# State space tables from low powers and multiples of 16, for four pairs at once, in place of a doubling per two pairs

## The chip, the cores and the metric

The kernel is one program on one core of one Trainium2 chip. The metric is the device time of one execution in microseconds. Three runs of the kernel before took 2755.88, 2739.55 and 2752.0 us; their median, 2752.0 us, is the time to compare with.

## What is computed

The input is a residual stream x of 1024 tokens by 2048 columns, in float32, and the reference passes it through two layers. Layer 0 has one input projection, eight gating heads, eight heads of stick-breaking attention and an output projection. Layer 1 is a diagonal complex state space (S5) with a gated linear unit. Each layer is modulated by a conditioning vector and normed before and after.

Only layer 1's state space matters for the change. It has 64 groups of 16 channels with 64 complex states each:

```
a   = exp(lam * dt)                                   # per group and state, complex
h_t = a * h_(t-1) + (coef * b) u_t                    # scan over the 1024 tokens
y_t = Re(c h_t) + d_skip * u_t
```

The kernel works in chunks of 8 tokens, 128 of them. From one chunk to the next a state is multiplied by a^8, which is a magnitude and a turn e8 = exp(i * angle). The scan over chunks runs on real numbers after the states have been turned back; so it needs, for every state, the table of turns e8^n for n = 0 to 127, as cosine and sine. This table, called `et`, is what the change computes in another way.

## The kernel before

**The whole.** A scheduler sets the order of every engine's instructions from the order in which they are written, their dependencies and priorities; each engine then works through its own list strictly in order. TensorE (PE) is busy nearly all the time. Each projection is a float32 product made of three matmuls: `load_w` splits a raw weight chunk into a high part, which ScalarE (ACT) copies (`whi`, L180), and a low part, which VectorE (DVE) subtracts (`wlo`, L181), and `mm3` multiplies them (L206 to L208).

**Layer 0** loops over eight heads h (L623). A head has a projection `v`, every second one a projection `bz`, then `qk`, the attention, and `uz`. Attention (L540) is a chain of short steps for each block of 128 queries: scores `z` on PE, three functions on ACT, add (L557), masks on GpSimd (POOL, L559 and L572), a scan (L563) and a subtraction (L569) on DVE, an exponential on ACT, transposes on PE, their copy `wT` on DVE (L578), and the product `oT` on PE (L580). The attention of a head runs beside the `v` projection of the next.

**The preparation of layer 1** is spread through layer 0. The generator `s5_prep` is started after the attention of head 3, and from then on a loop takes its steps, by `NPREP`: 3 in head 3, 4 each in heads 4 to 6, 1 in head 7. As the scheduler sets them, they run beside the projections of heads 4 to 7. A step makes the matrices of two pairs of groups, so that there are 16 steps. In each:

- POOL loads `br`, `bi` and, in every second step, `cl`; DVE makes `bbr`, `bbi` and the block matrix `bd`.
- POOL multiplies them by powers of a (`gm`, `ga`, L1143 and L1146): `Tr` and `Ti`, then `cAr` and `cAi`. DVE ends `cAi` (L1210).
- `write_wb` transposes `Tr` and `Ti` of one pair on PE (`wb_ps`, L1215); DVE (L1217) and ACT (L1218) copy them into `wb`, and SP stores that. It is called for the first pair early, and for the second after the table.
- PE multiplies `bd` with `cAr` and `cAi` (`k_ps`, L1228 and L1230); DVE writes it beside 128 zeros into `kst`, and SP stores both halves into `kk_d`.
- DVE makes the table `et` by doubling: from m entries the next m are those times e8^m (`em`), 6 instructions for each of 7 levels, and 5 more to square `em` for each of the first 6. SP stores it by four DMAs into `et_d`.

All tiles of the preparation have one buffer; so the next step's `et` waits until the four DMAs of the last have read it.

Of the kernel before, what the change touches and what calls it, by code (L numbers as in the profile page):

```python
# [13 lines left out]
ALU = mybir.AluOpType  # L14
PSUM = bass.MemoryType.PSUM
# [10 lines left out]
class TableOrder:  # L26
    """Keeps the ScalarE functions that need different tables in separate runs."""

# [35 lines left out]
def hybrid_trunk(ctx: ExitStack, tc: tile.TileContext, x, c, ln_pre_g, ln_post_g, w_mod, b_mod,  # L64
# [27 lines left out]

# [1 line left out]
    cat_d = dram.tile([16, 128, L], F32, name="cat_d")  # L94
# [9 lines left out]

# [1 line left out]
    ident = const.tile([128, 128], F32, name="ident")  # L106
# [33 lines left out]
    def rstd_from(ss, n, cnt, pool, name):  # L140
        """1/sqrt(ss/cnt + eps) of a [128, n] tile: exp(-log/2), then one Newton step."""
        r = pool.tile([128, n], F32, tag=name, name=name)
        v = pool.tile([128, n], F32, tag=name + "v", name=name + "v")
        t = pool.tile([128, n], F32, tag=name + "t", name=name + "t")
        V.tensor_scalar(out=v, in0=ss, scalar1=1.0 / cnt, scalar2=EPS, op0=ALU.mult, op1=ALU.add)
        tab.act(r, v, AF.Ln)
        tab.act(r, r, AF.Exp, scale=-0.5)
        V.tensor_tensor(out=t, in0=r, in1=r, op=ALU.mult)
        V.tensor_tensor(out=t, in0=t, in1=v, op=ALU.mult)
        V.tensor_scalar(out=t, in0=t, scalar1=-0.5, scalar2=1.5, op0=ALU.mult, op1=ALU.add)  # L150
        V.tensor_tensor(out=r, in0=r, in1=t, op=ALU.mult)
        return r

    def col_sums(ps, acc, n):
        """[128, n*128] partial sums -> [128, n] PSUM columns."""
        for i in range(n):
          with hi_prio():
            T.matmul(ps[:, i:i + 1], acc[:, i * 128:(i + 1) * 128], ones, start=True, stop=True)
# [16 lines left out]

# [1 line left out]
    RAW, SUB = 1024, 512  # L177
# [5 lines left out]
    def load_raw(parts, ncols, dma=dma):  # L183
        """parts: (k, first column, DRAM slice [128, k, n]) -> raw tile [128, RAW]."""
        raw = wp.tile([128, RAW], F32, tag="wraw", name="wraw")
        rv = raw.rearrange("p (k n) -> p k n", n=ncols)
        for k, c0, src in parts:
            dma(out=rv[:, k:k + src.shape[1], c0:c0 + src.shape[2]], in_=src)
        return raw
# [3 lines left out]
    def load_w(parts, ncols, eng=V, raw=None, dma_=dma):  # L193
        """Yields the weight chunk in parts of SUB elements, split."""
        if raw is None:
            with hi_prio():
                raw = load_raw(parts, ncols, dma_)
        for i in range(RAW // SUB):
            with hi_prio():
                h = wp.tile([128, SUB], F32R, tag="whi", name="whi")  # L200
                lo = wp.tile([128, SUB], F32R, tag="wlo", name="wlo")
                split(h, lo, raw[:, i * SUB:(i + 1) * SUB], eng)
            yield h.rearrange("p (k n) -> p k n", n=ncols), lo.rearrange("p (k n) -> p k n", n=ncols)
# [6 lines left out]
    def gemm(nk, ncols, src, banks, evac, name, pre=None, eng=V):  # L210
        """src(k0, k1): parts of the weight rows; banks: (width, f), f(k, w_hi, w_lo) -> operands.

        k outermost, so that every weight chunk is used once; in the last chunk bank by bank."""
        ps = [mm_tile(name) for _ in banks]
# [17 lines left out]

# [1 line left out]
    w7 = w_in_ab[0].rearrange("(k p) (s n) -> p k s n", p=128, s=7)  # L234
# [25 lines left out]

# [1 line left out]
    # h^T starts without the shift: its part of the first projections is a bias, and the shift is added to h^T later.  # L262
    first = ((6, None), (3, 4), (0, 2))
# [156 lines left out]

# [1 line left out]
    with pool("pa") as pa, pool("pu") as pu_, pool("pst") as pst, pool("pat", 2) as pat, ExitStack() as pm_stack:  # L422
# [15 lines left out]
        def bias_first():  # L438
            """The shift's part of the first projections."""
            for gi, (s0, s1) in enumerate(first):  # L440
# [25 lines left out]
        def mod_chunk(layer, n0):  # L466
            """512 columns of silu(c) @ w_mod, as partial sums over partitions."""
            acc = pm.tile([128, 512], F32, tag="macc", name="macc")
# [31 lines left out]
        def sgu_scale(h):  # L500
            """Per-token norm of gelu(v) over the head, in the exp/log run."""
            av = st["av"]
# [92 lines left out]
        def gate_a(h):  # L595
            """Gates of gating head h, with gelu of the next head's v."""
            tab.begin("silu")
# [66 lines left out]

# [1 line left out]
    h1h = [None, None]  # L666
# [3 lines left out]
    def pairs(ap, k0, cols):  # L670
        """Rows KORD[k0], KORD[k0 + 1] of ap [128, k, n], in one part if adjacent."""
        a, b = KORD[k0], KORD[k0 + 1]
        if b == a + 1:
            return [(0, 0, ap[:, a:a + 2, cols])]
        return [(i, 0, ap[:, k:k + 1, cols]) for i, k in enumerate((a, b))]
# [82 lines left out]

# [1 line left out]
    wi = w_in_ssm[0].rearrange("(k p) n -> p k n", p=128)  # L760
# [130 lines left out]

# [1 line left out]
    yTh = big_tile(1, [128, 8, L], F32R, "yTh")  # L893
# [34 lines left out]

# [1 line left out]
    with pool("pd") as pd:  # L930
# [55 lines left out]
def s5_prep(nc, tc, tab, const, pst, ps_t, ps_o, ident, dma, lam_re, lam_im, b_re, b_im, c_re, c_im,  # L986
            d_skip, log_dt, wb_d, wc_d, kk_d, et_d):
    """Matrices of the state space for chunks of 8 steps; a generator, two pairs of groups per step.

    Rows (g2 p): the 64 states of the two groups of a pair."""  # L990
    V, S, G, T = nc.vector, nc.scalar, nc.gpsimd, nc.tensor
# [4 lines left out]
    def small(shape, name):  # L996
        cnt[0] += 1
        return pools[0].tile(shape, F32, tag=f"s5{name}", name=f"s5{name}{cnt[0]}")
# [152 lines left out]
    s5b = ExitStack()  # L1151
    pools[0] = s5b.enter_context(tc.tile_pool(name="s5b", bufs=1, reuse_waits="tile"))
    for bq in range(32 // NP):
        p0 = bq * NP
        b, g0 = p0 // 4, (p0 % 4) * 2
        psl = slice(p0, p0 + NP)
        if p0 % 4 == 0:
            cl = small([128, 2, 64], "cl")
# [67 lines left out]
        for r in range(NP):  # L1226
# [4 lines left out]
                     start=False, stop=True)  # L1231
            kst = small([32, 256], "kst")
            V.memset(kst[:, 0:128], 0.0)
            V.tensor_copy(kst[:, 128:256], pk)
            V.scalar_tensor_tensor(out=kst[:, 128:144], in0=eye2, scalar=dcol[:, p0 + r:p0 + r + 1],
                                   in1=kst[:, 128:144], op0=ALU.mult, op1=ALU.add)
            dma(out=kk_d[2 * (p0 + r):2 * (p0 + r) + 2].rearrange("g c x -> (g c) x"), in_=kst)
        et = small([128, NP, 2, 128], "et")
        em = small([128, 2, NP, 1], "em")
        tc_ = small([128, NP, 64], "tc")  # L1240
        V.memset(et[:, :, 0, 0:1], 1.0)
        V.memset(et[:, :, 1, 0:1], 0.0)
        V.tensor_copy(em[:, 0, :, 0], e8[:, 0, psl])
        V.tensor_copy(em[:, 1, :, 0], e8[:, 1, psl])
        m = 1
        while m < 128:
            emr, emi = (em[:, i].to_broadcast([128, NP, m]) for i in range(2))
            o_r, o_i = et[:, :, 0, m:2 * m], et[:, :, 1, m:2 * m]
            s_r, s_i = et[:, :, 0, 0:m], et[:, :, 1, 0:m]
            tt = tc_[:, :, 0:m]  # L1250
            mul(o_r, s_r, emr)
            mul(tt, s_i, emi)
            add(o_r, o_r, tt, ALU.subtract)
            mul(o_i, s_r, emi)
            mul(tt, s_i, emr)
            add(o_i, o_i, tt)
            if 2 * m < 128:
                e_r, e_i = em[:, 0], em[:, 1]
                x_, y_, w_ = tc_[:, :, 0:1], tc_[:, :, 1:2], tc_[:, :, 2:3]
                mul(x_, e_r, e_r)  # L1260
                mul(y_, e_i, e_i)
                mul(w_, e_r, e_i)
                add(e_r, x_, y_, ALU.subtract)
                add(e_i, w_, w_)
            m *= 2
        write_wb(1)
        for top in range(2):
# [33 lines left out]
```

## Time and profile before

| | |
|---|---|
| median of the runs, and their bounds | 2752.0 us, 2739.55 to 2755.88 |
| span of the profiled execution | 2749.7 us |
| that execution beside the median | 2.3 us under it, among the runs shown |
| PE busy | 2603.6 us (95%) |
| DVE busy | 1771.3 us (64%) |
| ACT busy | 1029.1 us (37%) |
| POOL busy | 491.7 us (18%) |

The profile has one execution. Its page gives busy time by engine and the chain of work that ended last; views of its trace give busy time by stretch, instructions in groups with the mean duration of one and the idle time before them, waits with what ended them, and instructions in order of time. PE's busy time counts a matmul from its start to its modelled end, and since the next starts before that end, a busy PE may still be waited on. The span is the sum's own time here; what lies around it is taken as the 2.3 us between it and the median.

### The profile page before, as it was taken

The numbers are of one execution on the slowest core, as the hardware profiler recorded it, in microseconds if no ns is written. First come the engines' busy times: TensorE is split into PE (matmuls) and PEld (weight loads), VectorE is DVE, ScalarE is ACT, GpSimd is POOL, SyncE is SP. The second block draws the span as 40 slices with busy tenths as digits, with TensorE's granted clock in tenths as the row PEclk, the third lists the DMA queues.
The fourth block names the chain that finished last, engine by engine and source line by source line (L and its number), as shares of the span: only waits on it lengthen the run. The fifth ranks groups of instructions, "written<-read, shape, count | busy, mean of one in ns | idle before, by whom it ended". The sixth has DMA issues, their size and how long they took to land.

```text
span 2749.7 us, 38891 instructions
## 1 busy us (share of the span) xinstructions
PE 2603.6 (95%) x13639; PEld 2184.9 (79%) x13639; DVE 1771.3 (64%) x4182; ACT 1029.1 (37%) x2035; POOL 491.7 (18%) x771
## 2 busy tenths in 40 slices
PE   4878999999999999999999999998999999999998
PEld 3657988988989878778888887787877888887876
DVE  7798877666766688888745464456364678546354
ACT  3444543333414314324434353444353222134332
POOL 2475000000001152340622400012030000002000
PEclk9989999999999999999999999999999999999999
DMA  8764656474571143332412235444254676454355
GB/s 287 270 208 124 203 164 198 146 238 147 184 238 56 58 111 83 100 95 62 141 54 90 86 100 181 153 156 135 93 183 150 207 222 191 132 186 158 126 194 170
DMA packets 356162, 417.97 MB, mean 152 GB/s; under 512 B 23632, under 2 KB 237952, under 8 KB 354560
## 3 DMA queue, kind: packets, MB, share of 16 engines
q1 hardware_dynamic: 346416, 392.95, 45.2%
q0 software_dynamic: 9552, 22.56, 2.5%
q8 instruction: 107, 1.75, 0.3%
q14 instruction: 87, 0.71, 0.1%
HBM read 355.62 MB, written 59.79 MB: 151 GB/s over the span
## 4 chain that ended last, share of the span: by engine, by line
PE 56%; DVE 20%; DMA 10%; issue 8%; ACT 4%; POOL 1%; SPq 1%; DVEq 0%; ACTq 0%; POOLq 0%
DVE wlo L181 2%; DMA mraw<-in_w_mod_dram 2%; DVE s5tc L1001 2%; DVE acc L174 2%; PE o0e L206 2%; PE o0e L208 2%; PE o0e L207 2%; PE o1e L206 2%; PE o1e L208 2%; PE o1e L207 2%; PE z L552 2%; PE oT L580 1%; DMA et_d<-s5et 1%; DVE y L732 1%; DMA wraw<-cat_d 1%
## 5 line engine op out<-in xcount | busy, mean ns | idle before, releaser
L180 ACT ACTIVATE whi<-wraw 128x512 fp32r<-128x512 f32 x632 | 395.1, 628 | 973.7 <-PE o1e L208 89.6
L181 DVE TENSOR_TENSOR wlo<-wraw,whi 128x512 fp32r<-128x512 f32 x592 | 423.4, 718 | 487.9 <-ACT whi L180 480.9
L174 DVE SCALAR_TENSOR_TENSOR macc<-mraw,cond,macc 128x512 f32<-128x512 f32 x240 | 180.1, 750 | 65.1 <-DMA mraw<-in_w_mod_dram 60.7
L207 PE MATMUL o1e<-wlo,catH 128*128 128x512 f32 x256 | 101.1, 395 | 3.9 <-DVE wlo L181 3.9
L207 PE MATMUL o0e<-wlo,catH 128*128 128x512 f32 x256 | 100.9, 394 | 0.0
L208 PE MATMUL o1e<-whi,catL 128*128 128x512 f32 x256 | 100.8, 394 | 0.0
L56 ACT ACTIVATE sp<-sp 128x128 f32<-128x128 f32 (+3 forms) x192 | 99.3, 521 | 3.7
L208 PE MATMUL o0e<-whi,catL 128*128 128x512 f32 x256 | 100.2, 393 | 0.0
L206 PE MATMUL o0e<-whi,catH 128*128 128x512 f32 x256 | 90.4, 396 | 6.8 <-ACT whi L180 3.9
L904 POOL TENSOR_TENSOR gt<-gt,zt 128x1024 f32<-128x1024 f32 x8 | 19.7, 2464 | 430.2 <-DMA gt<-g_d 430.2
L206 PE MATMUL o1e<-whi,catH 128*128 128x512 f32 x256 | 87.6, 393 | 2.2 <-ACT jk L704 2.0
L56 ACT ACTIVATE wt<-wt 128x128 f32<-128x128 f32 (+3 forms) x96 | 50.2, 523 | 104.8 <-DVE wt L569 93.0
L580 PE MATMUL oT<-wT,v 128*128 128x128 f32 x576 | 82.5, 280 | 5.9 <-DVE wT L578 5.9
L580 PEld LDWEIGHTS oT<-wT,v 128*128 128x128 f32 x576 | 76.4, 195 | 9.7 <-DVE wT L578 6.9
L735 POOL DMA_DIRECT2D x_d<-y x32 | 18.1, 566 | 368.7 <-DVE y L732 367.8
L56 ACT ACTIVATE sp<-z 128x128 f32<-128x128 f32 (+3 forms) x96 | 46.6, 487 | 88.2 <-PE z L552 87.1
L552 PE MATMUL z<-k,q 128*128 128x128 f32 (+3 forms) x192 | 78.2, 491 | 1.3 <-DVE wt L569 1.0
L174 DVE SCALAR_TENSOR_TENSOR acc<-m,cond,acc 128x512 f32<-128x512 f32 x60 | 72.8, 1213 | 8.0 <-DMA m<-in_w_mod_dram 6.7
L559 POOL TENSOR_SCALAR_AFFINE_SELECT sp<-sp 128x128 f32<-128x128 f32 x64 | 25.0, 390 | 279.8 <-DVE sp L557 216.2
L181 POOL TENSOR_TENSOR wlo<-wraw,whi 128x512 fp32r<-128x512 f32 x40 | 60.9, 1536 | 61.0 <-ACT whi L180 59.7
L1218 ACT ACTIVATE s5wb<-wb_ps 128x128 f32<-128x128 f32 x64 | 17.8, 277 | 140.7 <-DVE s5wb L1217 122.0
L578 DVE COPY wT<-wT_ps 128x128 f32<-128x128 f32 (+3 forms) x96 | 53.0, 553 | 21.0 <-PE wT_ps L576 20.6
(627 smaller groups left out, 8206.5 us busy)
## 6 DMA issues: line engine op xcount, KB each, us to landing
wraw<-in_w_in_ab_dram SPq DMA_DIRECT2D x268, 256.0 KB, 3.3
mraw<-in_w_mod_dram SPq DMA_DIRECT2D x256, 256.0 KB, 3.4
wraw<-in_w_in_ssm_dram SPq DMA_DIRECT2D x56, 512.0 KB, 4.5
wraw<-in_w_out_ab_dram SPq DMA_DIRECT2D x48, 512.0 KB, 3.8
raw<-in_w_mod_dram SPq DMA_DIRECT2D x16, 1024.0 KB, 6.6
m<-in_w_mod_dram SPq DMA_DIRECT2D x32, 512.0 KB, 4.5
wraw<-in_w_out_ssm_dram SPq DMA_DIRECT2D x32, 512.0 KB, 3.8
wraw<-in_w_in_ab_dram SPq DMA_DIRECT2D x17, 512.0 KB, 4.9
```

The costliest lines, as they stand in the source:

```text
L56: r = self.nc.scalar.activation(out, in_, func, **kw)
L174: V.scalar_tensor_tensor(out=acc, in0=m, scalar=cond[:, k:k + 1], in1=acc, op0=ALU.mult, op1=ALU.add)
L180: S.activation(h, r, AF.Copy)
L181: eng.tensor_tensor(out=lo, in0=r, in1=h, op=ALU.subtract)
L206: T.matmul(ps, sh, mh, start=first, stop=False)
L207: T.matmul(ps, sh, ml, start=False, stop=False)
L208: T.matmul(ps, sl, mh, start=False, stop=last)
L552: T.matmul(z[:, :w], q[:, i * 128:(i + 1) * 128], kT[:, k0:k1], start=True, stop=True)
L578: V.tensor_copy(wT[:, :w], pt[:, :w])
L580: T.matmul(oT, v[:, k0 // 128 + j, :], wT[:, j * 128:(j + 1) * 128], start=nb_done == 0, stop=nb_done == i)
L732: V.scalar_tensor_tensor(out=y[:, qs], in0=y[:, qs], scalar=r, in1=xr, op0=ALU.mult, op1=ALU.add)
L1001: V.tensor_tensor(out=o, in0=a, in1=b, op=ALU.mult)
```

## The change

The table is made in two stages. `powers` runs once for four pairs, in every second step: it makes e8^n for n = 0 to 15 (`fin`) by four levels of doubling, and then the multiples e8^(16 k) for k = 0 to 7 (`crs`) by three more. `cmul` runs in every step, and multiplies `fin` and `crs` out to the 128 entries of `et`: 6 instructions of 128 elements for each of the two pairs. Its scratch tile is `Tr`, which the transposes of `write_wb` have then to have read; `write_wb` of the second pair is written ahead of it now. The 128 zeros of `kk_d` are stored once, by eight DMAs ahead of the steps, from a tile in the place of `cl`; `kst` keeps its right half alone. Comments and docstrings were removed elsewhere, which moves no instruction.

```diff
+    def powers(p0):
+        fin, crs = small([128, 2, 4, 16], "fin"), small([128, 2, 4, 8], "crs")
+        em, tp = small([128, 2, 4, 1], "em"), small([128, 4, 8], "tp")
+        V.tensor_copy(em[:, :, :, 0], e8[:, :, p0:p0 + 4])
+        for t, n in ((fin, 16), (crs, 8)):
+            V.memset(t[:, 0, :, 0:1], 1.0)
+            V.memset(t[:, 1, :, 0:1], 0.0)
+            m = 1
+            while m < n:
+                emr, emi = (em[:, i].to_broadcast([128, 4, m]) for i in range(2))
...
+                mul(o_r, s_r, emr)
+                mul(tt, s_i, emi)
+                add(o_r, o_r, tt, ALU.subtract)
+                mul(o_i, s_r, emi)
+                mul(tt, s_i, emr)
+                add(o_i, o_i, tt)
...
+                mul(x_, e_r, e_r)
+                mul(y_, e_i, e_i)
+                mul(w_, e_r, e_i)
+                add(e_r, x_, y_, ALU.subtract)
+                add(e_i, w_, w_)
+                m *= 2
+        return fin, crs
+    def cmul(o_r, o_i, fin, crs, tmp):
+        shp = [128, 8, 16]
...
+        for r in range(NP):
+            tt = tmp[:, r]
+            f_r, f_i = (fin[:, i, r].unsqueeze(1).to_broadcast(shp) for i in range(2))
+            c_r, c_i = (crs[:, i, r].unsqueeze(2).to_broadcast(shp) for i in range(2))
+            mul(v3(o_r[:, r]), f_r, c_r)
+            mul(tt, f_i, c_i)
+            add(v3(o_r[:, r]), v3(o_r[:, r]), tt, ALU.subtract)
+            mul(v3(o_i[:, r]), f_r, c_i)
+            mul(tt, f_i, c_r)
+            add(v3(o_i[:, r]), v3(o_i[:, r]), tt)
+    zero = small([128, 2, 64], "cl").rearrange("p a b -> p (a b)")
+    V.memset(zero, 0.0)
+    for i in range(8):
+        dma(out=kk_d[8 * i:8 * i + 8, :, 0:128].rearrange("g c x -> (g c) x"), in_=zero)
     for bq in range(32 // NP):
         p0 = bq * NP
...
+        if p0 % 4 == 0:
+            efin, ecrs = powers(p0)
...
-            kst = small([32, 256], "kst")
-            V.memset(kst[:, 0:128], 0.0)
...
+            kst = small([32, 128], "kst")
...
+        write_wb(1)
         et = small([128, NP, 2, 128], "et")
-        em = small([128, 2, NP, 1], "em")
-        tc_ = small([128, NP, 64], "tc")
...
-        m = 1
-        while m < 128:
...
-            if 2 * m < 128:
...
-            m *= 2
-        write_wb(1)
+        cmul(et[:, :, 0, :], et[:, :, 1, :], efin[:, :, p0 % 4:p0 % 4 + NP], ecrs[:, :, p0 % 4:p0 % 4 + NP], Tr)
```

The scheduler's lists differ from the first preparation step in head 4 to the last, early in layer 0's output projection; ahead of it and behind it they are the same on every engine. Three places follow, all on DVE. `s5et`, `s5em` and `s5tc` are the table, the squared turn and the scratch of the doubling; `s5fin`, `s5crs` and `s5Tr` are the two factors and the scratch of the product. The change's rows bear its own line numbers: L1271 is what L1217 was, L1287 what L1234 was, L1288 what L1235 was, L1238 what L1184 was, L1242 what L1188 was.

The first place is the attention of head 4 beside the projection `v` of head 5. Before:

```order
L584 TENSOR_TENSOR bz_8984<-oT,bz_8984 128x16x8
L1001 TENSOR_TENSOR s5et_10407<-s5et_10407,s5em_10408 128x2x32
L1001 TENSOR_TENSOR s5tc_10409<-s5et_10407,s5em_10408 128x2x32
L1001 TENSOR_TENSOR s5et_10407<-s5et_10407,s5em_10408 128x2x32
L578 COPY wT<-wT_ps 128x512
L1004 TENSOR_TENSOR s5et_10407<-s5et_10407,s5tc_10409 128x2x32
L535 TENSOR_TENSOR sg<-sg,u 128x1024
L1001 TENSOR_TENSOR s5tc_10409<-s5et_10407,s5em_10408 128x2x32
L181 TENSOR_TENSOR wlo<-wraw,whi 128x512
L536 TENSOR_TENSOR u<-sg,zg 128x128x8
```

The same place in the change:

```order
L569 TENSOR_TENSOR wt<-z,wt 128x512
L181 TENSOR_TENSOR wlo<-wraw,whi 128x512
L584 TENSOR_TENSOR bz_8962<-oT,bz_8962 128x16x8
L578 COPY wT<-wT_ps 128x512
L535 TENSOR_TENSOR sg<-sg,u 128x1024
L181 TENSOR_TENSOR wlo<-wraw,whi 128x512
L536 TENSOR_TENSOR u<-sg,zg 128x128x8
```

Before, the doubling stands between the copies `wT`, the scans and the low halves `wlo`; in the change nothing of the table stands there.

The second place is the one just behind it, where the fourth step's table is made in the change:

```order
L1001 TENSOR_TENSOR s5Tr_9800<-s5fin_8020,s5crs_8021 128x128
L1271 COPY s5wb_9829<-wb_ps 128x2x64
L1004 TENSOR_TENSOR s5et_9865<-s5et_9865,s5Tr_9800 128x128
L1001 TENSOR_TENSOR s5Tr_9800<-s5fin_8020,s5crs_8021 128x128
L1004 TENSOR_TENSOR s5et_9865<-s5et_9865,s5Tr_9800 128x128
L181 TENSOR_TENSOR wlo<-wraw,whi 128x512
```

These are the real and then the imaginary part of the first pair's product. The first row writes `Tr`, and so has to follow PE's transposes of it; `wlo` stands behind it on the same engine. Before, POOL alone wrote `Tr`, and DVE had no such instruction.

The third place is the same point one and a half rounds later, behind the attention of head 6, beside the projection `v` of head 7. Before:

```order
L584 TENSOR_TENSOR bz_12760<-oT,bz_12760 128x16x8
L1217 COPY s5wb_14125<-wb_ps 128x2x64 x2
L181 TENSOR_TENSOR wlo<-wraw,whi 128x512
L1234 COPY s5kst_14141<-k_ps 32x128
L1235 SCALAR_TENSOR_TENSOR s5kst_14141<-s5eye_7532,s5dcol_7531,s5kst_14141 32x16
```

And in the change:

```order
L1287 COPY s5kst_13926<-k_ps 32x128
L1238 MEMSET s5bd_14066 128x128
L1004 TENSOR_TENSOR s5fin_13956<-s5fin_13956,s5tp_13959 128x4
L1004 TENSOR_TENSOR s5em_13958<-s5tp_13959 128x4
L1288 SCALAR_TENSOR_TENSOR s5kst_13926<-s5eye_7532,s5dcol_7531,s5kst_13926 32x16
L1242 COPY s5bd_14066<-s5bbr_14059 64x2x16 x2
L1001 TENSOR_TENSOR s5tp_13959<-s5fin_13956,s5em_13958 128x4
```

Before, the doubling has long run ahead of its steps and is over here; in the change the table is made in its own step, and DVE has powers and products in head 7 too. Counted from one L535 to the next (each gating head has one, at the end of an attention), the doubling has 73 instructions up to that of head 3, then 446, 604, 93 and none, 1216 in all; the change has 74, then 133, 227, 197, 209 and 8, which is 848.

## Rows read from the trace of the kernel before

**Rows 1.** Stretches, heads 1 to 7: length, then PE, PEld, DVE, ACT, POOL busy; clock; DMA.
```profile
309.60:470.70 161.10, 161.10 (x964) 141.48 (x963) 121.21 (x206) 67.08 (x145) 10.39 (x25) 1.00 0.62 193
470.70:682.30 211.60, 210.04 (x1196) 181.92 (x1195) 143.82 (x237) 77.83 (x157) 8.83 (x25) 1.00 0.56 175
682.30:839.80 157.50, 154.54 (x922) 137.30 (x921) 102.81 (x163) 48.96 (x101) 3.52 (x8) 0.99 0.60 188
839.80:1054.80 215.00, 210.69 (x1160) 174.29 (x1159) 164.30 (x703) 74.53 (x164) 72.62 (x145) 1.00 0.28 78
1054.80:1240.50 185.70, 174.06 (x982) 143.54 (x981) 153.37 (x714) 67.70 (x154) 62.98 (x137) 0.98 0.33 92
1240.50:1466.30 225.80, 221.37 (x1222) 185.92 (x1221) 148.63 (x572) 88.58 (x186) 67.28 (x138) 0.99 0.29 83
1466.30:1633.00 166.70, 165.47 (x969) 140.30 (x968) 89.18 (x202) 69.72 (x155) 54.26 (x116) 1.00 0.32 95
```

**Rows 2.** Groups of PE, 839 to 1633 us: count | busy us, mean ns | idle before.
```profile
L1228 PE MATMUL k_ps<-s5cAr,s5bd 128*32 128x128 f32 x60 | 12.1, 283 | 4.0 <-DVE s5kst L1234 1.5 <-DVE s5bd L1188 1.2 <-DVE s5tc L1001 0.6
...
L1215 PE MATMUL wb_ps<-ident,s5Tr 128*128 128x128 f32 x30 | 8.6, 285 | 2.9 <-POOL s5cAr L1146 0.9 <-DVE s5em L1004 0.7 <-issue 0.6
...
L1165 PE MATMUL c_ps<-ident,s5cl 128*128 128x128 f32 x8 | 2.3, 285 | 1.4 <-ACT s5wb L1218 1.4
```

**Rows 3.** The chain that ended last, 840 to 1633 us: shares by line.
```profile
by line: DVE s5tc L1001 6.8%; DMA et_d<-s5et 4.6%; DVE wlo L181 3.9%; DVE s5et L1004 3.7%; issue 3.5%; DVE s5et L1001 3.3%; PE z L552 2.5%; DVE wt L563 2.4%; PE oT L580 2.3%; DVE s5em L1004 2.1%; PE v4e L206 1.9%; PE v4e L207 1.9%; PE v4e L
```

**Rows 4.** Waits, 900 to 1560 us: total us, times, longest us.
```profile
ACT s5wb L1218 <- DVE s5wb L1217: 120.2, 44, 8.3
POOL s5Tr L1143 <- PE wb_ps L1215: 65.9, 4, 22.7
...
DVE s5et L1241 <- DMA et_d<-s5et: 30.6, 13, 5.5
```

**Rows 5.** Waits of PE, 900 to 1400 us, the longest of 16.
```profile
PE oT L580 <- DVE wT L578: 5.2, 4, 2.4
```

**Rows 6.** Waits in head 7, 1466 to 1633 us.
```profile
POOL s5Tr L1143 <- PE wb_ps L1215: 20.7, 2, 19.3
ACT s5wb L1218 <- DVE s5wb L1217: 12.6, 10, 3.7
```

**Rows 7.** Groups of DVE that the change removes or replaces, 840 to 1633 us.
```profile
L1004 DVE TENSOR_TENSOR s5et<-s5et,s5tc 128x2 f32<-128x2 f32 (+6 forms) x224 | 51.1, 228 | 2.2
L1001 DVE TENSOR_TENSOR s5et<-s5et,s5em 128x2 f32<-128x2 f32 (+6 forms) x224 | 49.6, 224 | 0.5
L1001 DVE TENSOR_TENSOR s5tc<-s5et,s5em 128x2 f32<-128x2 f32 (+6 forms) x224 | 48.4, 216 | 2.0
L1001 DVE TENSOR_TENSOR s5tc<-s5em 128x2 f32<-128x2 f32 x288 | 43.3, 190 | 2.6
L1004 DVE TENSOR_TENSOR s5em<-s5tc 128x2 f32<-128x2 f32 x192 | 27.6, 175 | 2.3
...
L1233 DVE MEMSET s5kst<- 32x128 f32 x31 | 5.1, 165 | 16.9 <-DMA kk_d<-s5kst 14.3 <-DMA wb_d<-s5wb 2.4
```

**Rows 8.** The doubling's groups, shapes apart, 840 to 1560 us: five of 21.
```profile
L1004 DVE TENSOR_TENSOR s5et<-s5et,s5tc 128x128 f32<-128x128 f32 x32 | 10.5, 328 | 0.2
...
L1001 DVE TENSOR_TENSOR s5et<-s5et,s5em 128x128 f32<-128x128 f32 x32 | 9.8, 306 | 0.0
...
L1001 DVE TENSOR_TENSOR s5et<-s5et,s5em 128x32 f32<-128x32 f32 x32 | 8.0, 250 | 0.0
...
L1001 DVE TENSOR_TENSOR s5et<-s5et,s5em 128x8 f32<-128x8 f32 x32 | 7.1, 223 | 0.0
...
L1001 DVE TENSOR_TENSOR s5tc<-s5et,s5em 128x2 f32<-128x2 f32 x32 | 5.3, 165 | 0.0
```

**Rows 9.** DVE in order of time, in head 4's attention: start us, us.
```profile
1062.14 0.16 DVE L1001 TENSOR_TENSOR s5tc<-s5et,s5em 128x2 f32<-128x2 f32 x1
1062.22 0.15 DVE L1001 TENSOR_TENSOR s5et<-s5et,s5em 128x4 f32<-128x4 f32 x1
```

More of the change, by code (lines that the diff above doesn't have):

```diff
@@ L1152, in s5_prep, with v3 @@
     pools[0] = s5b.enter_context(tc.tile_pool(name="s5b", bufs=1, reuse_waits="tile"))
+    def powers(p0):
[8 more added lines that the diff above has]
+                emr, emi = (em[:, i].to_broadcast([128, 4, m]) for i in range(2))
+                o_r, o_i = t[:, 0, :, m:2 * m], t[:, 1, :, m:2 * m]
+                s_r, s_i = t[:, 0, :, 0:m], t[:, 1, :, 0:m]
+                tt = tp[:, :, 0:m]
+                mul(o_r, s_r, emr)
[4 more added lines that the diff above has]
+                add(o_i, o_i, tt)
+                e_r, e_i = em[:, 0], em[:, 1]
+                x_, y_, w_ = tp[:, :, 0:1], tp[:, :, 1:2], tp[:, :, 2:3]
+                mul(x_, e_r, e_r)
[7 more added lines that the diff above has]
+        shp = [128, 8, 16]
+        def v3(t):
+            return t.rearrange("p (a b) -> p a b", b=16)
+        for r in range(NP):
[12 more added lines that the diff above has]
+        dma(out=kk_d[8 * i:8 * i + 8, :, 0:128].rearrange("g c x -> (g c) x"), in_=zero)
     for bq in range(32 // NP):
@@ L1231, in s5_prep @@
                      start=False, stop=True)
-            kst = small([32, 256], "kst")
-            V.memset(kst[:, 0:128], 0.0)
[L1234 to L1237, printed above, removed]
-        et = small([128, NP, 2, 128], "et")
-        em = small([128, 2, NP, 1], "em")
-        tc_ = small([128, NP, 64], "tc")
[L1241 to L1244, printed above, removed]
-        m = 1
-        while m < 128:
[L1247 to L1256, printed above, removed]
-            if 2 * m < 128:
[L1258 to L1264, printed above, removed]
-            m *= 2
-        write_wb(1)
+            kst = small([32, 128], "kst")
+            V.tensor_copy(kst, pk)
+            V.scalar_tensor_tensor(out=kst[:, 0:16], in0=eye2, scalar=dcol[:, p0 + r:p0 + r + 1],
+                                   in1=kst[:, 0:16], op0=ALU.mult, op1=ALU.add)
+            dma(out=kk_d[2 * (p0 + r):2 * (p0 + r) + 2, :, 128:256].rearrange("g c x -> (g c) x"), in_=kst)
+        write_wb(1)
+        et = small([128, NP, 2, 128], "et")
+        cmul(et[:, :, 0, :], et[:, :, 1, :], efin[:, :, p0 % 4:p0 % 4 + NP], ecrs[:, :, p0 % 4:p0 % 4 + NP], Tr)
         for top in range(2):
```

## The prediction

> **What bounds the kernel now.** I read the stretches of the heads first, since the preparation lies in heads 4 to 7 alone. [Rows 1]: PE is busy in nearly all of every stretch, so it sets the pace. Heads alternate between long ones with a `bz` projection (2, 4, 6) and short ones (1, 3, 5, 7). By head 2, and by the mean of heads 1 and 3 (161.1 and 157.5, so 159.3), heads 4 to 7 should take 2 x 211.6 + 2 x 159.3 = 741.8 us. They take 215.0 + 185.7 + 225.8 + 166.7 = 793.2. The surplus of 51.4 us (3.4, 26.4, 14.2 and 7.4 by head) is what the preparation costs. Most of it is in head 5, which also has the lowest clock, 0.98, and the most PE idle time, 185.7 - 174.06 = 11.6 us.
>
> Part of the surplus is PE's own work for the preparation. [Rows 2] give 12.1 us for `k_ps` of L1228 and 8.6 for `wb_ps` of `Tr`; those of L1230 and of `Ti` are alike, and `c_ps` is 2.3: at most 43.7 us, by durations. Matmuls overlap, so I take half, 22, as the estimate of what they occupy, and 43.7 as the upper bound. So 8 to 29 us are left as stalls that DVE, ACT or POOL cause.
>
> Second, the chain of waits. [Rows 3]: in these heads the doubling's lines lead it (`s5tc` 6.8%, `s5et` 3.7 and 3.3, `s5em` 2.1), and the wait for the DMA that empties `et` has 4.6%. That chain is of the preparation itself, whose end layer 1 needs only much later; so its shares are no gain. They show that the doubling is what paces the preparation on DVE.
>
> Third, who waits for DVE. [Rows 4]: ACT waits 120.2 us for a copy that DVE makes into `wb`, because that copy stands in DVE's list among the doubling. ACT's next work, the high halves `whi`, then comes late, and PE after it. PE's own longest wait for DVE is `wT`, 5.2 us in four times [rows 5]: the copies that the first place of the order shows amid the doubling. In head 7, where the doubling is over, ACT's same wait is 12.6 us [rows 6] and PE's idle 166.7 - 165.47 = 1.2 [rows 1].
>
> **The change, part by part.** *Removed.* The five groups of the doubling are 51.1 + 49.6 + 48.4 + 43.3 + 27.6 = 220.0 us and the memset of `kst` 5.1 [rows 7], together 225.1 us of DVE, in 1216 + 31 instructions.
>
> *Added.* `powers` has seven levels of 6 instructions and 5 for the square behind each: 77, of which 6 handle 128x32 and 36 smaller tiles. A 128x32 costs 250 ns [rows 8]; the small ones stand between 165 and 223 [rows 8], and I take 190; a square is three of 190 and two of 175 [rows 7], 0.92 us. That is 6 x 0.25 + 36 x 0.19 + 7 x 0.92 = 14.8 us, eight times 118. `cmul` has 12 instructions in each of 16 steps, 128 products and 64 sums of 128 elements: 128 x 0.306 + 64 x 0.328 [rows 8] = 60 us. Together 178 us; copies and memsets that start a table stand on both sides and are left out.
>
> *Balance.* 225 - 178 = 47 us less of DVE, by durations. These overlap: two neighbours start 80 ns apart and take 160 and 150 [rows 9], so the time freed is between half of it, 23, and all, 47. One instruction of the table has on average 220.0 / 1216 = 0.181 us before, and 178 / 848 = 0.210 now.
>
> [...]
>
> *Moved.* More than the total, the place counts. From one L535 to the next, the counts that follow the orders give 446 x 0.181 - 133 x 0.210 = 53 us less DVE work in the interval that ends early in head 5, and 604 x 0.181 - 227 x 0.210 = 61 less in the next, which covers most of head 5; then 197 x 0.210 - 93 x 0.181 = 24 more, and 209 x 0.210 = 44 more in the last, in head 7. So heads 4 and 5 are relieved where PE stalls most, and head 7 pays, where DVE is busy for only 89.18 of 166.7 us [rows 1]; with 44 more it would be at 133, 80%, about what head 5 has before (153.37 of 185.7, 83%).
>
> *The wait for `et`'s DMA* (30.6 us in 13 times [rows 4]). It ends DVE's idle time at the start of a table. The product writes `et` much later after the previous DMA in every second step, the one that makes powers first (14.8 us); I take half, 15 us, as gone. It is part of the same stalls, not a second gain. *The scratch `Tr`* adds a wait of DVE for PE's transposes, with `wlo` behind it (second place); as forecast it ends before DVE is there, since `write_wb` of the second pair is now written ahead; else see the third rival. *Eight DMAs of zeros* (64 KB each) go out once on SP's queue between two weight loads: hidden, as DMA has a share of 0.28 in head 4 [rows 1]; uncovered, a weight chunk is late once, by no more than the longest wait for a DMA in [rows 4], 5.5 us. *The memset of `kst`* waited 14.3 us for a DMA [rows 7], and the copy in its place waits likewise: nothing. *POOL's wait for the zeros in `cl`* comes once: nothing, as POOL is busy 62.98 of 185.7 us [rows 1].
>
> **The sum.** What DVE's relief can give back is PE idle time in heads 4 and 5: 4.3 + 11.6 = 15.9 us. In heads 1 to 3 PE was idle 0 + 1.6 + 3.0 of 530.2 us, 0.86%; the same share of the 400.7 us of heads 4 and 5 is 3.4, so 12.5 us go. The clock of 0.98 in head 5 goes to 1.00, as in head 4: 0.02 x 185.7 = 3.7. Head 7 loses some 2 us to its busier DVE (its idle rises from 1.2 to the 3 of head 3). 12.5 + 3.7 - 2 = 14 us. The profiled execution goes from 2749.7 us to about 2735.7; with the 2.3 us that it lies under the median, 2752.0 - 14 = **2738 us**.
>
> **The rivals.**
> *The whole stall goes.* PE's transposes and products are half hidden in the stalls that others cause, and all 25 to 29 us of stall, those of head 6 too, fall. For it: the surplus of 26.4 in head 5 is far over its idle time, so stalls lie in PE's busy time too. Against: the steps remain, with the same transposes on PE. 2723 to 2727 us.
>
> *Nothing.* The preparation is then paced by POOL's products and PE's transposes, and whatever instructions DVE still has among the attention delay `wT` and `wlo` just as well, but in heads 6 and 7. For it: 53 + 61 relieved and 24 + 44 paid back is two thirds moved rather than removed, and the smallest instructions, 165 to 190 ns, were not the long ones that a `wT` waits for. Against: head 7 has 1.2 us idle, so it has room. 2744 to 2757 us.
>
> *DVE takes over the wait for the transposes.* POOL waits 65.9 us for `wb_ps` in four times, up to 22.7 [rows 4], and 20.7 in head 7 [rows 6]: PE does the transposes when its list comes to them, between projections. The product's first use of `Tr` puts that wait on DVE, and `wlo` and `wT` behind it on PE. If all 65.9 move there and the gain stays: 2738 + 66 = 2804; if half, 2771. It decides when PE is not done with `wb_ps` as DVE reaches the product. Against: powers and the `k_ps` copies stand between in every second step, and `write_wb` comes earlier than before.
>
> *The clock alone stays.* The 0.98 in head 5 is what these projections get and not what stalls cause: 3.7 us less gain, 2742. That lies inside the forecast's own range.
>
> **How the numbers follow.** The forecast, with its own range of 2730 to 2743, gets 0.50; the whole stall 0.16; nothing 0.26; DVE's new wait 0.08. To hold 8 in 10, the range takes in most of the first rival and all of "nothing", and leaves out the third: 2720 to 2758. About 1%, 27 us, is what a measurement of this kernel can tell from no change, its runs being 16 us apart: faster by more means under 2724.5, half of the first rival and some of the forecast's tail, 0.15. Slower by more means over 2779.5, the worse half of the third rival and unnamed mishaps, 0.05. The rest, 0.80, is within.
>
> **What would show it.** Heads 4 and 5 without rows of the doubling in the attention, ACT's wait at `s5wb` down from 120.2 to some 50 us (four heads like head 7), head 5 near 170 us with 4 us of PE idle and a clock of 1.00, and head 7 at 168 to 170. The first step that fails would be this: head 5 stays at 180 or more though DVE's busy time there fell by some 40 us; then DVE was not what held PE. The third rival would show as idle time of DVE before the product into `s5Tr`, ended by PE `wb_ps`, and the second as PE idle in heads 6 and 7 that grows by what heads 4 and 5 lose. [...]

## The result and the profile after

The changed kernel takes 2725.03 us, median of five runs (2723.2 to 2728.97), beside 2752.0 before; the ratio is 0.9915, 95% interval 0.9895 to 0.9934. That is 27 us faster, where 14 was forecast: inside the range, at the time of the first rival (2723 to 2727). The profiled execution has a span of 2726.2 us.

The heads 4 to 7 in the changed kernel, which answer to the last four of [rows 1]: length, then PE, PEld, DVE, ACT, POOL busy; clock; DMA.

```profile
841.10:1049.90 208.80, 208.80 (x1159) 174.76 (x1158) 140.48 (x530) 76.52 (x168) 70.52 (x147) 1.00 0.29 82
1049.90:1219.20 169.30, 169.26 (x989) 142.00 (x988) 122.95 (x416) 70.13 (x159) 65.04 (x137) 1.00 0.31 91
1219.20:1437.40 218.20, 217.73 (x1214) 183.29 (x1213) 136.96 (x434) 84.92 (x179) 65.03 (x135) 1.00 0.28 80
1437.40:1605.30 167.90, 165.93 (x968) 140.23 (x967) 118.60 (x403) 69.17 (x155) 54.62 (x116) 1.00 0.37 106
sum 764.20, PE 761.72 PEld 640.29 DVE 519.00 ACT 300.74 POOL 255.21; mean PE 190.43 PEld 160.07 DVE 129.75 ACT 75.18 POOL 63.80
```

764.2 us instead of 793.2: 29.0 less, by head 6.2, 16.4 and 7.6 less and, in head 7, 1.2 more. PE's idle time fell from 21.6 to 2.5 us, its busy time by 9.9. The clock went from 0.98 and 0.99 to 1.00 in heads 5 and 6, which by an estimate from these rows and [rows 1], with busy time taken to go as one over the clock, accounts for 0.02 x 174 + 0.01 x 221 = 5.7 of the 9.9 (the rows give the clock to 0.01, so this is good to some 2 us). The lists outside heads 4 to 7 and the start of `o0e` are the same; there this execution happens to be 5.5 us longer, so that the span fell by 23.5.

What PE waited for in heads 4 to 6 of the kernel before (839.8 to 1466.3 us), total, times, longest:

```profile
PE oT L580 <- DVE wT L578: 5.2, 4, 2.4
PE sgw L518 <- ACT s5wb L1218: 3.1, 1, 3.1
PE k_ps L1230 <- DVE s5cAi L1210: 2.3, 4, 0.7
PE k_ps L1228 <- DVE s5kst L1234: 1.5, 1, 1.5
PE c_ps L1165 <- ACT s5wb L1218: 1.4, 2, 1.2
PE k_ps L1228 <- DVE s5bd L1188: 1.2, 1, 1.2
```

With ten smaller ones these are 20.2 us. Only 5.2 are the attention's `wT` and none is a projection's `wlo`. 10.6 us are the preparation's own matmuls (`k_ps`, `c_ps` and `wb_ps`; 6.4 in the rows above, 4.2 in seven of the smaller ones): they stand at fixed places in PE's list, and when DVE or ACT brings their inputs late (`cAi`, `kst`, `bd`), the projection behind them waits too. `sgw`, 3.1 us, is a transposition of a gating head, and no work of the preparation; but it shares the one buffer of the pool `ps_t` (L84) with `wb_ps`, `c_ps` and `wT_ps`, and so waits, like `c_ps`, until ACT has copied `wb` out of it. In the changed kernel the same view of heads 4 to 6 has one row:

```profile
PE v6e L207 <- DVE wlo L181: 0.5, 1, 0.5
```

Other waits of the changed kernel, 900 to 1560 us, which answer to [rows 4]:

```profile
ACT s5wb L1272 <- DVE s5wb L1271: 103.8, 48, 7.5
...
DVE s5et L1001 <- DMA et_d<-s5et: 17.9, 7, 4.1
...
DVE s5Tr L1001 <- PE wb_ps L1269: 3.6, 4, 1.2
```

And DVE's groups of the new table, 830 to 1620 us, which stand where [rows 7] stood: busy us, mean ns, idle before.

```profile
L1001 DVE TENSOR_TENSOR s5tp<-s5em 128x4 f32<-128x4 f32 x168 | 28.4, 207 | 1.5
...
L1004 DVE TENSOR_TENSOR s5et<-s5et,s5Tr 128x128 f32<-128x128 f32 x60 | 20.1, 337 | 0.6
L1001 DVE TENSOR_TENSOR s5Tr<-s5fin,s5crs 128x128 f32<-128x128 f32 x60 | 18.7, 311 | 4.1 <-PE wb_ps L1269 3.6
L1001 DVE TENSOR_TENSOR s5et<-s5fin,s5crs 128x128 f32<-128x128 f32 x64 | 17.8, 324 | 18.0 <-DMA et_d<-s5et 17.9
```

The product's instructions took 311 to 337 ns (306 and 328 were put in), and wait 3.6 us for PE's transposes. In the multiplications the broadcast of `crs` repeats each word and that of `fin` a run of 16; they took 311 and 324 ns, and the sums of plain operands 337. So no cost of the repeats shows here, and none shows before, where the product with the repeated `em` took 306 ns beside 328 for the sum [rows 8].

### The profile page after: what moved, and what is told of

Read it like the earlier page. It is cut to its first block, busy times and chain, and to the rows that moved or that the text cites. A ratio compares the mean times of both kernels' runs of the same rounds, so it can differ in the third digit from the quotient of the medians.

```text
span 2726.2 us, 38501 instructions
## 1 busy us (share of the span) xinstructions
PE 2595.3 (95%) x13639; PEld 2180.4 (80%) x13639; DVE 1733.9 (64%) x3783; ACT 1029.2 (38%) x2035; POOL 487.8 (18%) x771
## 4 chain that ended last, share of the span: by engine, by line
PE 68%; DVE 11%; DMA 8%; issue 8%; ACT 3%; POOL 1%; SPq 0%; DVEq 0%; ACTq 0%; POOLq 0%
PE oT L580 2%; PE z L552 2%; DVE acc L174 2%; DMA mraw<-in_w_mod_dram 2%; PE o0e L206 2%; PE o1e L206 2%; PE o1e L208 2%; PE o1e L207 2%; PE o0e L208 2%; PE o0e L207 2%; DVE wlo L181 1%; DMA xr<-in_x_dram 1%; DMA wraw<-cat_d 1%; PE su1e L206 1%; PE wT_ps L576 1%
## 5 line engine op out<-in xcount | busy, mean ns | idle before, releaser
L735 POOL DMA_DIRECT2D x_d<-y x32 | 17.9, 561 | 369.7 <-DVE y L732 368.3
L557 DVE SCALAR_TENSOR_TENSOR sp<-z,sp 128x128 f32<-128x128 f32 (+3 forms) x96 | 52.9, 551 | 31.6 <-ACT sp L56 31.5
```

The costliest lines, as they stand in the source:

```text
L557: V.scalar_tensor_tensor(out=a[:, :w], in0=z[:, :w], scalar=0.0, in1=a[:, :w], op0=ALU.max, op1=ALU.add)
```

## The experiments

Two questions led them. What of the 29 us is the smaller load of DVE, and what the shorter wait for the DMAs that read `et`? And is it the amount of DVE's work, its place, or its form? Lengths are of heads 4 to 7 in the profiled execution, and DVE is its busy time there; ratios are to the kernel before, each in runs beside it on one chip, with 95% intervals. A length comes from one execution, and these lay between 3.8 us under (E10) and 8.0 us over (E14) the median of their kernel; so a few us between two lengths tell nothing by themselves. Heads 5 and 6 are best taken together: by the rows' counts, up to some 15 matmuls fall on one side of their border or the other.

| kernel | ratio | heads 4 to 7 | DVE |
|---|---|---|---|
| before | 1 | 793.2 | 555.5 |
| the change | 0.9915 [0.9895, 0.9934] | 764.2 | 519.0 |
| no table (E1) | 0.9941 [0.9923, 0.9958] | 774.6 | 394.7 |
| no table, no wait (E10) | 0.9893 [0.9876, 0.9909] | 764.3 | 389.7 |
| change, no wait (E9) | 0.9921 [0.9898, 0.9944] | 767.8 | 523.6 |
| change, scratch in `tb` (E7) | 0.9913 [0.9897, 0.9929] | 763.9 | 522.4 |
| change, product twice (E5) | 0.9950 [0.9930, 0.9971] | 776.6 | 562.1 |
| change, powers in every step (E6) | 0.9972 [0.9956, 0.9988] | 782.3 | 603.1 |
| before, no wait (E8) | 0.9977 [0.9965, 0.9989] | 783.6 | 555.3 |
| E8, doubling to 64 (E14) | 0.9998 [0.9984, 1.0012] | 787.2 | 535.9 |
| before, zeros once (E2) | 1.0003 [0.9985, 1.0020] | 793.7 | 555.1 |
| doubling behind `k_ps`, no wait (E13) | 1.0025 [1.0012, 1.0039] | 789.8 | 567.2 |
| doubling behind `k_ps` (E12) | 1.0027 [1.0013, 1.0040] | 784.2 | 563.9 |
| doubling, scratch in `Tr` (E11) | 1.0056 [1.0035, 1.0077] | 764.3 | 513.6 |

**E1, no table.**

```diff
-            efin, ecrs = powers(p0)
...
-        cmul(et[:, :, 0, :], ...)
+        V.memset(et, 0.0)
```

> The changed kernel with powers and the product left out: et is only set to zero, so the turns are missing from the output, and 178 us of DVE by the prediction's prices are gone. Theory A (the change took away everything that the table cost PE; what is left of the preparation's surplus, 22.6 of 51.4 us, is PE's own transposes and products): within 4 us of the changed kernel's 2725.0, heads 4 to 7 at 760 to 766 us as there (764.2). Rival B (the table still costs: DVE's remaining 178 us delay PE in proportion, as 225 us cost 27 us more than now): 10 to 20 us less, 2705 to 2715, heads 4 to 7 near 745.

Neither: 2733 us, no faster than the change though 124 us of DVE's work are gone, and 10 us longer in heads 4 to 7. The loss is in one head, 219.4 us in head 4; the others are 171.6, 217.1 and 166.5. The memset depends on nothing but its buffer, so all 16 run ahead into head 4, and wait there for the last step's DMAs: 36.2 us, all in that head. E10 takes this up.

**E2, the zeros alone.**

```diff
+        dma(out=kk_d[8 * i:8 * i + 8, :, 0:128].rearrange("g c x -> (g c) x"), in_=zero)
...
-            V.memset(kst[:, 0:128], 0.0)
```

> The kernel before with one part of the change alone: the zeros of kk_d are stored once by eight DMAs, and kst keeps its right half. The doubling stays. Theory A (the gain is the table's alone): as before, 2745 to 2756 us, heads 4 to 7 near 793. Rival Z (the memset of kst, which waited 16.9 us for DMAs on DVE, and the halved stores held DVE and what stands behind it): a third of the gain or more, 2743 or less, with heads 4 to 7 under 785.

As theory A said: 2751.75. The halved stores and the memset are worth nothing that shows. The other side part, `write_wb` of the second pair written ahead, leaves every engine's list as it was when put into the kernel before alone, so it wasn't run.

**E5, the product twice.**

```diff
-        cmul(et[:, :, 0, :], ...)
+        for _ in range(2):
+            cmul(et[:, :, 0, :], ...)
```

> The changed kernel with every product done twice over (192 more instructions of 128 elements, 60 us of DVE): DVE's work for the table is then 238 us, 13 more than the doubling's 225, in 1040 instructions. Theory T (DVE's total time for the table decides): the gain is gone, 2748 to 2760, heads 4 to 7 near 793. Rival C (what decides is how closely small instructions crowd the attention and the preparation's own copies in heads 4 and 5; the added work is spread evenly, up to 269 instructions from one L535 to the next instead of 572): at most a third is lost, 2725 to 2734, heads 4 to 7 at 764 to 773.

Between: 2735.4, 12.4 us more in heads 4 to 7: 13.6 more in heads 5 and 6 together, and a little less in the others. DVE is as busy as before the change, and half of the gain stays. Heads 4 and 6:

```profile
844.50:1053.10 208.60, 208.60 (x1159) 174.75 (x1158) 149.90 (x564) 75.33 (x166) 71.62 (x145) 1.00 0.29 82
1225.90:1454.20 228.30, 222.22 (x1229) 186.70 (x1228) 152.62 (x495) 90.33 (x190) 73.70 (x141) 0.99 0.27 77
```

**E6, powers in every step.**

```diff
-        if p0 % 4 == 0:
-            efin, ecrs = powers(p0)
+        efin, ecrs = powers(p0 // 4 * 4)
```

> The changed kernel with powers made in every step in place of every second (616 more small instructions, 118 us of DVE): the table is then 1424 instructions without the starting ones and 296 us, more than the doubling's 1152 and 225, but spread: 281, 369, 343 and 354 from one L535 to the next, where the doubling had 422, 572, 89 and none. Theory T (total time decides): slower than before, 2755 to 2785, with head 7 longer by 10 or more. Rival C (crowding in one place decides, and 369 is between the 213 that cost nothing and the 572 that stalled): between the two kernels, 2730 to 2745, heads 4 to 7 at 769 to 784.

2743, as rival C put it, so making the powers for four pairs at once is a part that counts: without it 18 of 29 us are lost. Here 84 us more of DVE cost 18 in the heads, and 43 in E5 cost 12; with the scatter of single executions, whether the loss is proportional to the added work can't be told.

**E8, E9, E10, no wait for `et`.** Each has the same edit to the stores of the table; E10 is E1 without its memset as well.

```diff
-                    in_=et[h * 64:(h + 1) * 64].rearrange("p r a n -> p r (a n)"))
+                    in_=pw[h * 64:(h + 1) * 64].rearrange("p a b c -> p (a b c)")[:, 0:512].rearrange("p (r x) -> p r x", r=NP))
```

> The kernel before with the whole doubling kept, but its four DMAs per step read 512 constants of another tile instead of et (the turns are missing from the output); so the next doubling never waits until et has been read. DVE's work is unchanged, 225 us; its wait at the start of a table, 30.6 us in 13 times, is gone. Theory W (a good part of the gain of the change is that its product reaches et later, with 17.9 us of waits left in 7 times: while DVE waits there, wlo, wT and the copies of wb stand behind it): 2730 to 2740, heads 4 to 7 at 773 to 783. Theory L (the load of DVE's table instructions among the attention is the cause, and the wait a symptom that costs nothing): as before, 2745 to 2754, heads 4 to 7 at 790 or more.

> The changed kernel with the same edit: the four DMAs read a constant tile, and the product never waits for them (17.9 us in 7 times are gone). Theory W: not slower, and up to 6 us faster, 2719 to 2726, since PE has only 2.5 us of idle time left in heads 4 to 7 (764.2 us). Theory L: as the changed kernel, 2723 to 2730.

> The changed kernel without any table (no powers, no product, no memset of et; the turns are missing) and with the four DMAs from a constant tile. Beside the kernel that kept the memset of et (2733.2 us, heads 4 to 7 at 774.6, 36.2 us of waits for the DMAs in 12 times, head 4 at 219.4) it takes away those waits alone. Theory W: head 4 falls back to 208 to 210 and heads 4 to 7 to 762 to 766, 2719 to 2726. Theory L (with hardly any load left, the rest is the list order of the preparation's copies and transposes): 2729 to 2736, head 4 still at 215 or more.

E8: 2742.15, 9.6 us less in heads 4 to 7, a third of the change's gain and just short of what theory W said. But not the wait alone went: with the stores no longer tied to `et`, the scheduler lets the doubling run further ahead. Heads 4 to 6 of E8, where DVE has 786, 845 and 359 instructions instead of 703, 714 and 572:

```profile
836.20:1053.80 217.60, 210.60 (x1159) 174.19 (x1158) 175.62 (x786) 74.03 (x164) 69.15 (x144) 1.00 0.39 106
1053.80:1233.20 179.40, 172.24 (x979) 142.02 (x978) 169.45 (x845) 67.65 (x153) 64.19 (x137) 0.99 0.26 75
1233.20:1453.20 220.00, 219.39 (x1222) 184.65 (x1221) 121.03 (x359) 88.54 (x187) 65.56 (x138) 1.00 0.25 73
```

Head 4 became longer and heads 5 and 6 shorter, so the 9.6 us hold the wait and the new place together. E9, whose table stays in its place: nothing beyond the scatter. E10: 2720.8, and head 4 is back as theory W said. Heads 4 to 7 of E10, the rows' columns as above:

```profile
837.70:1046.50 208.80, 208.80 (x1159) 174.82 (x1158) 109.25 (x323) 75.89 (x168) 69.79 (x147) 1.00 0.42 115
1046.50:1218.10 171.60, 171.13 (x1001) 143.25 (x1000) 92.22 (x208) 72.78 (x162) 63.33 (x137) 1.00 0.26 77
1218.10:1435.20 217.10, 216.02 (x1201) 181.97 (x1200) 100.52 (x219) 84.03 (x176) 63.96 (x135) 1.00 0.24 71
1435.20:1602.00 166.80, 165.45 (x969) 140.24 (x968) 87.75 (x194) 69.86 (x155) 54.29 (x116) 1.00 0.32 94
```

764.3 us without a table, without its wait: the change's 764.2 is this floor, so that its table costs PE nothing that these lengths show (the ratios, 0.9893 and 0.9915, have overlapping intervals and leave room for some us). The floor lies 22 us over the 741.8 of heads without a preparation. Head 4 of E1 beside it, the wait that E10 took away, and what PE waited for most in heads 4 to 6 of E1:

```profile
844.80:1064.20 219.40, 213.47 (x1158) 177.70 (x1157) 114.69 (x339) 75.56 (x168) 70.70 (x147) 0.98 0.41 109
```

```profile
DVE s5et L1291 <- DMA et_d<-s5et: 36.2, 12, 5.6
```

```profile
PE k_ps L1282 <- DVE s5cAi L1262: 5.1, 2, 3.3
```

So twelve such waits within one head cost 10 us though DVE is busy for only 114.69 of its 219.4 us; the memsets themselves, which E10 leaves out as well, are 5 us of DVE. While DVE waits, its whole list stands still, the copies of `wb` and `cAi` among it, and PE waited 5.1 us for `cAi`. In the changed kernel the 17.9 us are spread over four heads, at most 6.2 in one.

**E7, the scratch in `tb`.**

```diff
-            tt = tmp[:, r]
+            tt = tmp[:, 0:8]
...
-        cmul(..., Tr)
+        cmul(..., tb)
```

> The changed kernel with the product's scratch in tb (POOL's own scratch) instead of Tr, so that DVE no longer waits for PE's transposes of Tr (3.6 us in the changed kernel); POOL waits for DVE's product instead. If the third rival of the prediction had a share in the result: faster by up to 4 us, 2720 to 2724. If it had none: 2722 to 2730. If POOL's wait for tb delays the next step: slower, over 2730.

2724.8: the wait for `Tr` had no share.

**E11, E12, E13, the doubling held in its step.** E11 takes the scratch from `Tr` and has `write_wb` of the second pair ahead of the table, E12 takes it from `bd`, E13 is E12 with the edit of E8.

```diff
-        tc_ = small([128, NP, 64], "tc")
+        tc_ = Tr.rearrange("p r a b -> p r (a b)")[:, :, 0:64]          # E11
+        tc_ = bd.rearrange("p i r g c -> p (i r g c)").rearrange("p (r m) -> p r m", r=NP)   # E12, E13
```

> The kernel before with the whole doubling, 1152 instructions and 225 us of DVE, but with its scratch taken from Tr as in the change (write_wb of the second pair ahead of it), so that no table can run ahead of its own step: by the order its instructions are spread over the intervals from L535 to L535 about as 216, 310, 266, 288 and 68 instead of 69, 422, 572, 89 and none ahead. Theory C (the crowding in heads 4 and 5 is the cause: the same work spread out costs little): 2725 to 2736, heads 4 to 7 at 765 to 776. Theory T (the amount of DVE work is the cause; with the product done twice, 238 us and spread, heads 4 to 7 took 776.7, and powers in every step, 296 us, took 782.3): 2736 to 2745, heads 4 to 7 at 776 to 785. The waits for et's DMAs, up to 30 us, come with either. If the longer chain of each step, now behind its transposes, holds PE: 2750 or more, with head 7 longer by 10.

> The kernel before with the whole doubling, its scratch now taken from bd, which PE's k_ps has then to have read: again no table can run ahead of its step (216, 306, 270, 288 and 70 instructions from L535 to L535), but unlike with Tr, POOL does not wait for the end of a table (there it waited 101 us in 15 times, 70 instead of 38 of the last attention's products came behind the start of o0e, and the kernel took 2762). If that wait of POOL was what made that kernel slow: 2730 to 2748. If a doubling that stands in every step, also in head 7 and in the last steps, is slow by itself: 2755 or more, with 50 or more products of the last attention behind the start of o0e.

> The same kernel with the four DMAs of a step reading a constant tile, so that no wait for et is left (the turns are missing): 225 us of doubling, spread, and nothing else. Theory C (the crowding in heads 4 and 5 made the rest of the loss): 2722 to 2732. Theory T (the amount of DVE work in small instructions made it; the doubling run ahead, without the wait, took 2742): 2736 to 2748. By the waits alone it should be 5 to 10 us under its twin with the wait.

All three are slower than before, by 0.3 to 0.6%. E11 has a fault of its own: POOL, which also masks the attention, waits for each table's end,

```profile
POOL s5Tr L1143 <- DVE s5et L1004: 101.0, 15, 16.5
```

so that 70 instead of 38 products of the last attention come behind the start of `o0e`, which takes 233.7 us instead of 194.4. Its 764.3 us for the heads are no floor, then. E12 has no such wait of POOL and, in the stretch of `o0e`, 836 matmuls (842 before, 906 in E11); neither E12 nor E13 fits what was expected of them. E12 has `o0e` at 207.5 us, and why is open. Spread out, the doubling costs 20 to 26 us over the floor in heads 4 to 7, against 19 where it runs ahead without the wait (E8). Theory C, that crowding alone was the fault, falls. Nor did E13 come out 5 to 10 us under its twin E12, but at 2757.8 beside 2755.3: taking this wait away gained nothing here,

```profile
DVE s5et L1241 <- DMA et_d<-s5et: 13.3, 5, 4.0
```

where it was less than half as long as before. Heads 4 to 7 of E12:

```profile
839.40:1050.80 211.40, 209.45 (x1158) 174.84 (x1157) 143.78 (x549) 75.02 (x164) 70.12 (x141) 1.00 0.27 77
1050.80:1228.40 177.60, 170.90 (x988) 142.96 (x988) 137.70 (x528) 69.69 (x160) 63.01 (x142) 0.99 0.32 91
1228.40:1454.10 225.70, 218.94 (x1214) 185.06 (x1213) 150.32 (x539) 86.62 (x181) 64.46 (x137) 0.99 0.27 78
1454.10:1623.60 169.50, 166.14 (x968) 140.07 (x967) 132.05 (x506) 68.95 (x155) 54.05 (x116) 1.00 0.37 106
```

**E14, the doubling to 64 entries,** on E8.

```diff
-        while m < 128:
+        while m < 64:
```

> The kernel before with the doubling stopped at 64 entries and the four DMAs reading a constant tile: the last level of 6 instructions of 128 elements is left out in each of 16 steps (the turns are missing), 96 instructions and about 30 us of DVE. The small dependent instructions, 1056 of them, stay, and run ahead in heads 4 and 5 as before. Its twin with all 128 entries took 2742 us, with DVE busy for 555 us in heads 4 to 7 and these at 783.6; the changed kernel had 519 us and 764.2, the one with no table 390 us and 764.2. Theory T (a knee in DVE's total work, between 524 and 555 us): DVE near 525, heads 4 to 7 at 764 to 772, 2722 to 2732. Theory F (the form: a long chain of small dependent instructions, whatever its total): heads 4 to 7 at 778 or more, 2737 to 2743.

No gain: 2747.3. DVE came to 535.9 us and not near 525, so this run alone leaves theory T's knee standing; but with more DVE work, 562.1 us, E5 took 776.6 us in the heads where E14 took 787.2, so DVE's sum over the four heads is not what decides. The rows show why the sum was the wrong measure (heads 4 to 6):

```profile
845.90:1066.50 220.60, 213.40 (x1162) 175.67 (x1160) 176.94 (x827) 74.54 (x165) 68.31 (x146) 0.99 0.39 105
1066.50:1247.40 180.90, 172.60 (x987) 141.50 (x986) 164.04 (x836) 69.32 (x162) 62.71 (x138) 1.00 0.27 77
1247.40:1466.20 218.80, 217.26 (x1213) 183.55 (x1212) 105.40 (x229) 85.22 (x178) 66.86 (x135) 1.00 0.24 71
```

The doubling depends on nothing in its step but its buffer; so with fewer levels it ran further ahead. Heads 4 and 5 stay at 176.94 and 164.04 us of DVE, and at 12 and 9 over the floor; head 6, with 105.40, is 1.7 over it. The lengths are as theory F said and the time is 4 us over it, but with no less work in heads 4 and 5 this doesn't test the form.

## Why the prediction came out as it did

**The direction and its cause were right, the size was half.** That the doubling's load on DVE in heads 4 to 6 costs PE time is shown by E10 (no table: the floor), and by E5 and E6, where load put back takes time back. That the time lies within the range is owed to its width, which took in the first rival. The sizes of the DVE terms held: powers measured 117 us (118 forecast), the product 57 us in 184 instructions (60 in 192), and the wait for `et` fell by 12.7 us to 17.9 (by 15). DVE's busy time fell by 36.5 us, between the two bounds of 23 and 47. One slip changed little: 220.0 us are the time of 1152 instructions, not of 1216, so that a mean is 0.191 us and not 0.181, and after the change 0.220 and not 0.210. The memset, the zeros and `Tr` were rightly put at nothing (E2, E7), and head 5 at 169.3 us with a clock of 1.00 is what was named; its PE idle time, forecast at 4 us, is 0.04.

**The step that failed is the sum's first term,** "what DVE's relief can give back is PE idle time in heads 4 and 5", 12.5 us down to a background of 0.86%. Three parts of it were too small. Heads 4 and 5 lost all idle time, 15.9 us. Head 6 had no term in the sum, and the interval counted for it was to pay; it gave 7.6: 4.0 of idle time, and the rest in busy time. And stalls lie in PE's busy time too, of which only head 5's clock was counted; head 4 lost 1.9 us there at the same clock. The first rival had it right that the whole stall of 29 us goes; the surplus left is 22 us, the value taken for PE's own work. But that value was half of 43.7 us with no row for the half, so that it came out is luck, and that the 22 us are PE's own work is not shown.

**The head that pays was misplaced.** The counts ran from one L535 to the next and were read nearly as heads. In the stretches of [rows 1], DVE's busy time fell by 23.8, 30.4 and 11.7 us in heads 4 to 6 and rose by 29.4 in head 7, where +44 was forecast: a good part of the 604 instructions lay in head 6. Head 7 paid 1.2 us (2 forecast).

**The path named was mostly the wrong one.** ACT's wait for `wb` copies fell only to 103.8 us instead of some 50, and is 59.1 even with no table (E10, 900 to 1560 us):

```profile
ACT s5wb L1270 <- DVE s5wb L1269: 59.1, 43, 4.9
```

PE lost its idle time regardless. `wT` was 5.2 of 20.2 us, and no wait of PE in heads 4 to 6 ended with `whi`. The larger part, 10.6, were the preparation's own matmuls in PE's list; where ACT's copies of `wb` did hold PE (`sgw` and `c_ps`, 4.5 us), it was by the buffer that they share. What the DMA wait alone is worth differs by case: 10.3 us with 36.2 us of it in one head (E1 against E10, the memsets gone with it), nothing that shows with 17.9 us over four heads (E9) or 13.3 behind `k_ps` (E13). In the kernel before, wait and place together are 9.6 us (E8), a third of the gain; the other two thirds go with the table's work.

**What stays open** is how those two thirds divide by amount, form and place. DVE's busy time in a head does not order the losses. In head 4, where the floor is 208.8 us with 109.25 of DVE, E5 loses nothing with 149.90 (its row is above), but E6 loses 2.9 with 160.65, E13 6.2 with 146.88, and the kernel before 6.2 with 164.30:

```profile
841.80:1053.50 211.70, 209.24 (x1158) 174.53 (x1157) 160.65 (x690) 74.36 (x163) 69.45 (x144) 1.00 0.28 79
842.60:1057.60 215.00, 211.52 (x1159) 175.74 (x1158) 146.88 (x558) 73.75 (x163) 68.39 (x142) 0.99 0.39 107
```

E13 also ties the next step's `bd` to the end of the table, so it doesn't settle the form either.

## What to carry to other kernels

Where PE is nearly always busy, price a side task by heads with it against heads without it, and not by PE's idle time: the stall was larger, 29 us against 15.9 in the two heads priced, and the surplus less an estimate for the task's own matmuls had the right size here. Read what PE itself waits for, row by row, before naming a path; a side task's own small matmuls in PE's list (10.6 us of waits in heads 4 to 6 before), and buffers that it shares with the main work (3.1 us at `sgw`), pass its delays on. Less work did not help where the rest only ran further ahead into the same place (E14). Count moved work in the stretches whose time is to change, and look at the new order after an edit that was to take a wait away alone (E8).

## What was not expected

A kernel without the table (E1) was 10 us longer in heads 4 to 7 than one with it. Its memset waits on DVE for a DMA, 36.2 us in twelve times, all in head 4, and that cost 10 us of PE's time; the same kind of wait behind the powers, 17.9 us spread over four heads, cost none that shows (E9).
